# First MLP product with the high and the low part of its input side by side: one matmul of 512 columns and one of 256 in place of three of 256

## The chip, the core and the metric

The kernel runs on one core of a Trainium2 chip. A core has TensorE (matrix products out of SBUF into PSUM), VectorE and ScalarE (elementwise work), GpSimd, and SyncE, whose queue issues most of the loads. PSUM has 8 banks of 512 float32 values per partition. The metric is the device time of one execution in microseconds (us); the median of three runs of the kernel before is 319.94 us (319.66 to 320.01).

## What is computed

One decoder layer on 256 tokens of width 1024: a token mixer of three head groups behind one input projection, an output projection, then an MLP, and a last norm. The part that the change touches is the MLP:

```python
x = x + jnp.einsum('bse,ed->bsd', y, w_out[l])          # x: (1, 256, 1024)
h = rms_norm(x, norm_mlp[l])
u = jnp.square(jax.nn.relu(jnp.einsum('bsd,df->bsf', h, w_ff1[l])))   # w_ff1: (1024, 4096)
x = x + jnp.einsum('bsf,fd->bsd', u, w_ff2[l])          # w_ff2: (4096, 1024)
return rms_norm(x, norm_final)
```

All inputs are float32.

## The kernel before

**Precision.** TensorE multiplies float32 operands in a rounded form (fp32r, one column per cycle). To keep float32 accuracy every operand is split into a high part, rounded to fp32r by a ScalarE copy, and a low part, the difference that VectorE takes and rounds (`split`, lines 70 to 72). A product of two split operands is three matmuls into one PSUM region (`mm3`, lines 299 to 303): high by high, high by low, low by high. The first operand of `T.matmul(o, l, r)` after the output is the stationary one, loaded into the array by a weight load of its own before each matmul; the second is streamed, one column after the other.

**Order of the work.** The order on every engine is the order in which the program issues, written out by hand. The projections run as 84 slots (`slots`), with steps of other engines placed ahead of chosen slots (`plan`, from line 831). Input projection and output projection come first, then the MLP. All weights come in chunks of 128 x 2048 float32 (1 MB). `load` issues a chunk's DMA on SyncE's queue into one of three raw buffers, and `split_w` (line 96) casts half of it on ScalarE (`wh`) and takes the difference on VectorE (`wl`); the second half's split issues the load of three chunks further on. Four buffers each hold `wh` and `wl`.

**The MLP.** `evac_split` (line 171) writes the residual stream, transposed and scaled, as `x1h` and `x1l`: two tiles of 128 x 8 x 256, 8 depth tiles of 256 tokens. The hidden width of 4096 is worked off in 16 chunks of 256. The first product of chunk j (`ff1`, line 785) has, for each of two halves `c` of 128 hidden columns and each depth tile `k`, one `mm3` of 256 columns (`ff1_mm`): weight slice stationary, tokens streamed, both halves into one PSUM bank. `ff1_out` evicts it through `ff1_evac` (line 772): Relu and its Square, rounded to `uh`, on ScalarE, the unrounded square and the difference `ul` on VectorE. The second product (`ff2_mm`) has `uh` and `ul` as stationary operand and 512 columns of a second weight chunk streamed, four accumulators of one bank each held over all chunks. It is 24 matmuls of 512 columns per chunk against 48 of 256 columns in the first product.

Chunk 0 of the first product runs as the last four slots (`ff1_first`, in two banks) while the last transposes and splits of x1 come in; `ff1_first_out` evicts it. Then comes `ff1(1)`, and a loop over j (line 916): second product of j, split of two half chunks, first product of j + 2, split of two more, `ff1_out(j + 2)`. The second products of the last two chunks are done by `last_mm` (line 942) in another order, the last 24 of their matmuls with 256 columns, followed by the residual, the last norm and the stores.

`hTh` and `hTl` (line 155) are the same two parts for the input projection; `x1h` and `x1l` take over their memory.

Of the kernel before, what the change touches and what calls it, by code (L numbers as in the profile page):

```python
# [8 lines left out]
F32 = mybir.dt.float32  # L9
F32R = mybir.dt.float32r  # L10
I32 = mybir.dt.int32
AF = mybir.ActivationFunctionType
OP = mybir.AluOpType
AX = mybir.AxisListType

P = 128
S = 256
D = 1024
KT = D // P
# [13 lines left out]
def trunk_kernel(ctx: ExitStack, tc, x, x_t, w_in, w_out, w_ff1, w_ff2, small, hg_norm, norm_final, out):  # L33
    nc = tc.nc
    V, A, G, T = nc.vector, nc.scalar, nc.gpsimd, nc.tensor
# [12 lines left out]
    def mis(name):  # L48
        b = idle.pop(0)
        held[name] = (b,)  # L50
        return banks[:, b, :]
# [9 lines left out]
    def free(name):  # L61
        idle.extend(held.pop(name))

    def wt(name, shape, tag=None, bufs=None, dt=F32):
        return work.tile(shape, dt, name=name, tag=tag or name, bufs=bufs)

    def flat(t):
        return t.rearrange("p a b -> p (a b)")
# [83 lines left out]
        G.tensor_tensor(r, v, nhalf[:, 0:k], op=OP.pow)  # L152
        return r

    hTh = wt("hTh", [P, KT, S], tag="hTh", dt=F32R)
    hTl = wt("hTl", [P, KT, S], tag="hTl", dt=F32R)
    xsq = wt("xsq", [P, D], tag="yTh")
    gmix = sp[:, SP_GMIX:SP_GMIX + 8]

# [139 lines left out]
    def mm3(o, l, r, first, last):  # L299
        (lh, ll), (rh, rl) = l, r  # L300
        T.matmul(o, lh, rh, start=first, stop=False)  # L301
        T.matmul(o, lh, rl, start=False, stop=False)  # L302
        T.matmul(o, ll, rh, start=False, stop=last)  # L303
# [313 lines left out]
    ps_s, sc_t, nm_t, pr_t, ps_t, PT = {}, {}, {}, {}, {}, {}  # L617
# [110 lines left out]
        ts_ = slice(t * 128, (t + 1) * 128)  # L728
        big_mm(wacc[t, n], yTh[:, k, ts_], yTl[:, k, ts_], NI + k // 2, k % 2, n, k == 0, k == KT - 1)

    x1h = wt("x1h", [P, KT, S], tag="hTh", dt=F32R)
    x1l = wt("x1l", [P, KT, S], tag="hTl", dt=F32R)
    gmlp = sp[:, SP_GMLP:SP_GMLP + 8]
    x1ps = {}
    xt = xa[:, SP_WA:].rearrange("p (t d) -> p t d", t=2)
# [27 lines left out]
    FI = NI + 4  # L763
    uh, ul = {}, {}

    def ff1_mm(o, i, c, k):
        wh = hi_w[i].rearrange("p (k c) -> p k c", c=CW)
        wl = lo_w[i].rearrange("p (k c) -> p k c", c=CW)
        cs = slice(c * 128, (c + 1) * 128)
        mm3(o, (wh[:, k, cs], wl[:, k, cs]), (x1h[:, k, :], x1l[:, k, :]), k == 0, k == KT - 1)  # L770

    def ff1_evac(j, parts):
        r = wt("fr", [P, 512], tag="sc", bufs=3)
        u = wt("fu", [P, 512], tag="pr", bufs=2)
        uh[j] = wt("uh", [P, 512], tag="PT", bufs=8, dt=F32R)
        ul[j] = wt("ul", [P, 512], tag="PT", bufs=8, dt=F32R)
        for src, s_ in parts:
            A.activation(r[:, s_], src, AF.Relu)  # L778
            A.activation(uh[j][:, s_], r[:, s_], AF.Square)
            V.tensor_tensor(u[:, s_], r[:, s_], r[:, s_], op=OP.mult)  # L780
            V.tensor_tensor(ul[j][:, s_], u[:, s_], uh[j][:, s_].bitcast(F32), op=OP.subtract)

    ff1_ps = {}

    def ff1(j, i):
        ps = ff1_ps[j] = mis(f"f{j}")
        for c in range(2):
            for k in range(KT):
                ff1_mm(ps[:, c * 256:(c + 1) * 256], i, c, k)

    def ff1_out(j):
        ff1_evac(j, [(ff1_ps[j], slice(0, 512))])
        free(f"f{j}")

    facc = {}

# [4 lines left out]
        big_mm(facc[t, n], uh[j][:, cs], ul[j][:, cs], i, kk, n, j == 0 and kk == 0,  # L801
               (t, n) == (1, 1) and j == NF - 3 and kk == 1)

    f0 = {}

    def ff1_first(c, kg):
        if kg == 0:
            f0[c] = mis(f"f0{c}")[:, 0:256]
        for k in range(4 * kg, 4 * kg + 4):
            ff1_mm(f0[c], FI, c, k)  # L810

    def ff1_first_out():
        ff1_evac(0, [(f0[c], slice(c * 256, (c + 1) * 256)) for c in range(2)])
        free("f00")
        free("f01")

    def x1_ss():
        for t in range(2):
# [9 lines left out]
    slots += [(wout_part, k, t, n) for k in range(4) for t, n in tn]  # L828
    slots += [(wout_part, k, t, n) for t, n in tn for k in range(4, 8)]
    slots += [(ff1_first, c, kg) for kg in range(2) for c in range(2)]  # L830
    plan = {
        0: [(S_, 0, 0, 4), (x_split, 0), (x_split, 1)],
# [67 lines left out]
    for n, slot in enumerate(slots):  # L900
        for step in plan.get(n, ()):
            step[0](*step[1:])
        slot[0](*slot[1:])
    ff1_first_out()
    S_(FI + 2, 0)
    S_(FI + 2, 1)
    ff1(1, FI + 1)
    S_(FI + 3, 0)
    S_(FI + 3, 1)
    ff1_out(1)  # L910
    x1_ss()
    nc.sync.dma_start(nfb, bass.AP(tensor=norm_final.tensor, offset=norm_final.offset, ap=[[0, P], [1, D]]))
    i = FI + 2
    tnt = sorted(tn)
    tail = {}
    for j in range(NF):
        if j < NF - 2:
            for kk in range(2):
                for t, n in tnt:
                    ff2_mm(j, i, kk, t, n)  # L920
        else:
            tail[j] = i
        split_w(i + 2, 0)
        split_w(i + 2, 1)
        i += 1
        if j + 2 < NF:
            ff1(j + 2, i)
            split_w(i + 2, 0)
            split_w(i + 2, 1)
            ff1_out(j + 2)  # L930
            i += 1
# [136 lines left out]
```

## Time and profile before

| | before |
|---|---|
| median of 3 runs | 319.94 us (319.66 to 320.01) |
| the profiled execution's own time | 319.74 us |
| its span, first to last instruction | 318.0 us |
| mean granted TensorE clock | 0.995 of 2.4 GHz |
| TensorE matmul busy | 309.8 us (97%) |
| VectorE busy | 191.3 us (60%) |
| ScalarE busy | 171.9 us (54%) |

The profile is of one execution. Its times are microseconds from the start of the span unless marked ns. PE is TensorE's matmul, PEld its weight load, DVE is VectorE, ACT is ScalarE, SP is SyncE. L301 is line 301 of the kernel. Since most matmuls and splits go through helpers, their line is the helper's, and the tile names tell the stage: `banks<-x1h,wh` is the first product of the MLP, `banks<-wh,uh` the second, `banks<-wh,yTh` the output projection. Matmuls overlap in the pipeline and their ends are modelled, so the pace of a stretch is read from the starts.

### The profile page before, as it was taken

The numbers are of one execution on the slowest core, as the hardware profiler recorded it, in microseconds if no ns is written. First come the engines' busy times: TensorE is split into PE (matmuls) and PEld (weight loads), VectorE is DVE, ScalarE is ACT, GpSimd is POOL, SyncE is SP. The second block draws the span as 40 slices with busy tenths as digits, with TensorE's granted clock in tenths as the row PEclk, the third lists the DMA queues.
The fourth block names the chain that finished last, engine by engine and source line by source line (L and its number), as shares of the span: only waits on it lengthen the run. The fifth ranks groups of instructions, "written<-read, shape, count | busy, mean of one in ns | idle before, by whom it ended". The sixth has DMA issues, their size and how long they took to land.

```text
span 318.0 us, 5290 instructions
## 1 busy us (share of the span) xinstructions
PE 309.8 (97%) x2164; PEld 284.6 (89%) x2164; DVE 191.3 (60%) x287; ACT 171.9 (54%) x283; POOL 36.4 (11%) x83
## 2 busy tenths in 40 slices
PE   8999999999999999999999999999999999999991
PEld 7999999998999888999899889889989988988981
DVE  1848999983545493697635733753663573375363
ACT  3869699684595360686632652562463264256131
POOL 8328900021410000000000000000000000000000
PEclk9999999999999999999999999999999999999997
DMA  7996553360046346058566246337426624630003
GB/s 199 403 376 253 189 211 132 134 235 31 2 143 255 133 139 260 0 188 343 212 250 248 81 200 265 125 141 266 182 93 255 243 84 203 264 120 15 0 6 128
DMA packets 9961, 55.71 MB, mean 175 GB/s; under 512 B 1232, under 2 KB 1488, under 8 KB 4048
## 3 DMA queue, kind: packets, MB, share of 16 engines
q1 hardware_dynamic: 9216, 54.06, 45.3%
q10 hardware_dynamic: 720, 1.31, 1.3%
q8 instruction: 17, 0.28, 0.3%
q14 instruction: 8, 0.07, 0.1%
HBM read 54.32 MB, written 1.05 MB: 174 GB/s over the span
## 4 chain that ended last, share of the span: by engine, by line
PE 93%; DMA 2%; issue 2%; DVE 1%; ACT 0%; POOLq 0%; POOL 0%; ACTq 0%; DVEq 0%
PE banks L301 28%; PE banks L302 28%; PE banks L303 28%; PE banks L405 2%; DMA raw<-in_w_in_dram 2%; PE banks L641 1%; PE banks L659 1%; PE banks L168 1%; PE banks L676 1%; PE banks L675 1%; PE banks L458 1%; PE banks L521 1%; PE banks L674 1%; DVE xa L957 0%; PE banks L461 0%
## 5 line engine op out<-in xcount | busy, mean ns | idle before, releaser
L72 DVE TENSOR_TENSOR wl<-raw,wh 128x1024 fp32r<-128x1024 f32 (+1 forms) x100 | 113.4, 1181 | 20.1 <-ACT wh L71 18.5
L71 ACT CAST wh<-raw 128x1024 fp32r<-128x1024 f32 (+1 forms) x100 | 95.3, 1010 | 4.1 <-DMA raw<-in_w_in_dram 4.0
L301 PE MATMUL banks<-x1h,wh 128*128 128x256 f32 x256 | 72.4, 283 | 0.0
L302 PE MATMUL banks<-x1l,wh 128*128 128x256 f32 x256 | 72.4, 283 | 0.0
L303 PE MATMUL banks<-x1h,wl 128*128 128x256 f32 x256 | 72.4, 283 | 0.0
L778 ACT ACTIVATE fr<-banks 128x512 f32<-128x512 f32 (+1 forms) x17 | 9.7, 573 | 87.2 <-PE banks L303 87.2
L780 DVE TENSOR_TENSOR fu<-fr 128x512 f32<-128x512 f32 (+1 forms) x17 | 11.2, 659 | 69.5 <-ACT fr L778 69.5
L302 PE MATMUL banks<-wl,uh 128*128 128x512 f32 (+1 forms) x132 | 51.4, 389 | 0.0
L301 PE MATMUL banks<-wh,uh 128*128 128x512 f32 (+1 forms) x132 | 51.3, 389 | 0.0
L303 PE MATMUL banks<-wh,ul 128*128 128x512 f32 (+1 forms) x132 | 51.3, 389 | 0.0
L301 PEld LDWEIGHTS banks<-x1h,wh 128*128 128x128 f32 x256 | 49.0, 191 | 0.7
L302 PEld LDWEIGHTS banks<-x1l,wh 128*128 128x128 f32 x256 | 48.9, 191 | 0.7
L303 PEld LDWEIGHTS banks<-x1h,wl 128*128 128x128 f32 x256 | 49.0, 191 | 0.0
L301 PE MATMUL banks<-hTh,wh 128*128 128x256 f32 x128 | 37.7, 295 | 0.0
L302 PE MATMUL banks<-hTl,wh 128*128 128x256 f32 x128 | 36.6, 286 | 0.3 <-DVE hTl L162 0.3
L303 PE MATMUL banks<-hTh,wl 128*128 128x256 f32 x128 | 36.3, 284 | 0.0
L303 PEld LDWEIGHTS banks<-wh,ul 128*128 128x128 f32 x132 | 24.9, 188 | 5.7
L301 PEld LDWEIGHTS banks<-wh,uh 128*128 128x128 f32 x132 | 24.9, 189 | 5.0
L302 PEld LDWEIGHTS banks<-wl,uh 128*128 128x128 f32 x132 | 24.8, 188 | 5.1
L302 PEld LDWEIGHTS banks<-hTl,wh 128*128 128x128 f32 x128 | 24.6, 192 | 0.8 <-DVE hTl L162 0.8
L301 PEld LDWEIGHTS banks<-hTh,wh 128*128 128x128 f32 x128 | 24.6, 192 | 0.6 <-ACT hTh L161 0.2
L303 PEld LDWEIGHTS banks<-hTh,wl 128*128 128x128 f32 x128 | 24.6, 192 | 0.2 <-DVE wl L72 0.2
(198 smaller groups left out, 417.0 us busy)
## 6 DMA issues: line engine op xcount, KB each, us to landing
raw<-in_w_ff_dram SPq DMA_DIRECT2D x32, 1024.0 KB, 5.0
raw<-in_w_in_dram SPq DMA_DIRECT2D x10, 1024.0 KB, 5.9
raw<-in_w_out_dram SPq DMA_DIRECT2D x4, 1024.0 KB, 4.8
raw<-in_w_in_dram ACTq DMA_DIRECT2D x4, 256.0 KB, 7.3
xtok<-in_x_dram SPq DMA_DIRECT2D x2, 512.0 KB, 8.6
xa<-in_x_dram SPq DMA_DIRECT2D x2, 512.0 KB, 6.2
xa<-in_x_t_dram SPq DMA_DIRECT2D x3, 256.0 KB, 6.2
raw<-in_w_in_dram SPq DMA_DIRECT2D x2, 256.0 KB, 8.0
```

The costliest lines, as they stand in the source:

```text
L71: A.copy(hi, src)
L72: V.tensor_tensor(lo, src, hi.bitcast(F32), op=OP.subtract)
L168: T.transpose(pair[n % 2][:, i * 256 + t * 128:i * 256 + (t + 1) * 128], src[:, t, (k0 + n) * P:(k0 + n + 1) * P], ident)
L301: T.matmul(o, lh, rh, start=first, stop=False)
L302: T.matmul(o, lh, rl, start=False, stop=False)
L303: T.matmul(o, ll, rh, start=False, stop=last)
L405: T.matmul(ps[:, par, g * 64:(g + 1) * 64], kB[r, hp, hs], rhs, start=True, stop=True)
L458: T.matmul(dst, att_d[:, (hp * 2 + half) * 2 + par, :], bv[:, half, h * 64:h * 64 + 64], start=True, stop=(half == 0))
L521: T.matmul(ps[:, c * 256:(c + 1) * 256], spw[:, wofs + c * 128:wofs + (c + 1) * 128], xc[:, c, :], start=True, stop=True)
L641: T.matmul(ps_s[2 * pair + par][:, os], q[r, c, qs], k[r, c, ks], start=True, stop=True)
L778: A.activation(r[:, s_], src, AF.Relu)
L780: V.tensor_tensor(u[:, s_], r[:, s_], r[:, s_], op=OP.mult)
```

## The change

One tile holds the high and the low part of each depth tile next to each other: 128 x 8 x 2 x 256, for the input projection's `hT` and for the MLP's `x1c`; the old names become views of it. `ff1_mm` then needs two matmuls: the weight slice's high part against 512 columns (high and low tokens) into a whole bank, and its low part against the 256 high columns into the bank's first half. The product is the sum of the bank's two halves. `ff1_out` therefore copies the second half to SBUF on ScalarE and adds the first half to it on VectorE, for each of the two banks that a chunk now takes; VectorE computes max(s, 0) x s in one instruction, ScalarE rounds it to `uh`, VectorE takes the difference `ul`. Chunk 0 uses the same functions.

```diff
-    hTh = wt("hTh", [P, KT, S], tag="hTh", dt=F32R)
-    hTl = wt("hTl", [P, KT, S], tag="hTl", dt=F32R)
+    hT = wt("hT", [P, KT, 2, S], tag="hT", dt=F32R)
+    hTh, hTl = hT[:, :, 0, :], hT[:, :, 1, :]
...
-    x1h = wt("x1h", [P, KT, S], tag="hTh", dt=F32R)
-    x1l = wt("x1l", [P, KT, S], tag="hTl", dt=F32R)
+    x1c = wt("x1c", [P, KT, 2, S], tag="hT", dt=F32R)
+    x1h, x1l = x1c[:, :, 0, :], x1c[:, :, 1, :]
...
-        mm3(o, (wh[:, k, cs], wl[:, k, cs]), (x1h[:, k, :], x1l[:, k, :]), k == 0, k == KT - 1)
-
-    def ff1_evac(j, parts):
-        r = wt("fr", [P, 512], tag="sc", bufs=3)
-        u = wt("fu", [P, 512], tag="pr", bufs=2)
+        T.matmul(o, wh[:, k, cs], flat(x1c[:, k]), start=k == 0, stop=False)
+        T.matmul(o[:, 0:S], wl[:, k, cs], x1h[:, k, :], start=False, stop=k == KT - 1)
+
+    ff1_ps = {}
+
+    def ff1_out(j):
+        b = wt("fb", [P, 2, S], tag="sc", bufs=3)
+        s_ = wt("fs", [P, 2, S], tag="pr", bufs=2)
+        u = wt("fu", [P, 512], tag="sc", bufs=3)
         uh[j] = wt("uh", [P, 512], tag="PT", bufs=8, dt=F32R)
         ul[j] = wt("ul", [P, 512], tag="PT", bufs=8, dt=F32R)
-        for src, s_ in parts:
-            A.activation(r[:, s_], src, AF.Relu)
-            A.activation(uh[j][:, s_], r[:, s_], AF.Square)
-            V.tensor_tensor(u[:, s_], r[:, s_], r[:, s_], op=OP.mult)
-            V.tensor_tensor(ul[j][:, s_], u[:, s_], uh[j][:, s_].bitcast(F32), op=OP.subtract)
-
-    ff1_ps = {}
+        for c in range(2):
+            A.copy(b[:, c, :], ff1_ps[j, c][:, S:])
+        for c in range(2):
+            V.tensor_tensor(s_[:, c, :], ff1_ps[j, c][:, 0:S], b[:, c, :], op=OP.add)
+            free(f"f{j}{c}")
+        V.scalar_tensor_tensor(u, flat(s_), 0.0, flat(s_), op0=OP.max, op1=OP.mult)
+        A.copy(uh[j], u)
+        V.tensor_tensor(ul[j], u, uh[j].bitcast(F32), op=OP.subtract)
+
+    def ff1_part(j, i, c, ks):
+        if ks[0] == 0:
+            ff1_ps[j, c] = mis(f"f{j}{c}")
+        for k in ks:
+            ff1_mm(ff1_ps[j, c], i, c, k)
 
     def ff1(j, i):
-        ps = ff1_ps[j] = mis(f"f{j}")
-        for c in range(2):
-            for k in range(KT):
-                ff1_mm(ps[:, c * 256:(c + 1) * 256], i, c, k)
-
-    def ff1_out(j):
-        ff1_evac(j, [(ff1_ps[j], slice(0, 512))])
-        free(f"f{j}")
+        for c in range(2):
+            ff1_part(j, i, c, range(KT))
...
     def ff1_first(c, kg):
-        if kg == 0:
-            f0[c] = mis(f"f0{c}")[:, 0:256]
-        for k in range(4 * kg, 4 * kg + 4):
-            ff1_mm(f0[c], FI, c, k)
-
-    def ff1_first_out():
-        ff1_evac(0, [(f0[c], slice(c * 256, (c + 1) * 256)) for c in range(2)])
-        free("f00")
-        free("f01")
+        ff1_part(0, FI, c, range(4 * kg, 4 * kg + 4))
...
-    ff1_first_out()
+    ff1_out(0)
```

## Rows read from the trace of the kernel before

**Rows 1.** Page, part 1: engines' busy time, share of the span, instructions.
```profile
PE 309.8 (97%) x2164; PEld 284.6 (89%) x2164; DVE 191.3 (60%) x287; ACT 171.9 (54%) x283; POOL 36.4 (11%) x83
```

**Rows 2.** Page, part 4: the chain that ended last, shares by line.
```profile
PE banks L301 28%; PE banks L302 28%; PE banks L303 28%; PE banks L405 2%; DMA raw<-in_w_in_dram 2%; PE banks L641 1%; PE banks L659 1%; PE banks L168 1%; PE banks L676 1%; PE banks L675 1%; PE banks L458 1%; PE banks L521 1%; PE banks L674 1%; DVE xa L957 0%; PE banks L461 0%
```

**Rows 3.** Stages: length, busy PE, PEld, DVE, ACT, POOL; clock, DMA, GB/s.
```profile
152.52:158.13 5.61, 5.61 (x26) 4.52 (x25) 4.56 (x5) 5.02 (x6) 0.00 (x0) 1.00 0.41 171
158.13:163.88 5.75, 5.75 (x50) 5.75 (x49) 1.45 (x2) 0.00 (x0) 0.00 (x0) 1.00 0.94 362
141.16:300.20 159.04, 159.04 (x1011) 143.69 (x1010) 85.94 (x88) 72.47 (x88) 0.00 (x0) 1.00 0.48 182
```

**Rows 4.** Timeline, PE, one MLP round: start, duration; first of ff2, ff1, ff2.
```profile
152.52 0.39 PE L301 MATMUL banks<-wh,uh 128*128 128x512 f32 x1
...
158.13 0.28 PE L301 MATMUL banks<-x1h,wh 128*128 128x256 f32 x1
...
163.88 0.39 PE L301 MATMUL banks<-wh,uh 128*128 128x512 f32 x1
```

**Rows 5.** Timeline, PE, output projection: first and last of ten matmuls.
```profile
113.80 0.39 PE L302 MATMUL banks<-wl,yTh 128*128 128x512 f32 x1
...
115.84 0.39 PE L302 MATMUL banks<-wl,yTh 128*128 128x512 f32 x1
```

**Rows 6.** Timeline, PE, last stage: first and last of nine 256 wide matmuls.
```profile
308.63 0.28 PE L301 MATMUL banks<-wh,uh 128*128 128x256 f32 x1
...
309.56 0.28 PE L303 MATMUL banks<-wh,ul 128*128 128x256 f32 x1
```

**Rows 7.** Groups by line and shape: count | busy us, mean ns | idle before.
```profile
L778 ACT ACTIVATE fr<-banks 128x512 f32<-128x512 f32 x15 | 9.0, 598 | 87.2 <-PE banks L303 87.2
L779 ACT ACTIVATE uh<-fr 128x512 fp32r<-128x512 f32 x15 | 9.5, 634 | 0.5
L780 DVE TENSOR_TENSOR fu<-fr 128x512 f32<-128x512 f32 x15 | 10.4, 691 | 69.5 <-ACT fr L778 69.5
L781 DVE TENSOR_TENSOR ul<-fu,uh 128x512 fp32r<-128x512 f32 x15 | 10.4, 693 | 1.6
L71 ACT CAST wh<-raw 128x512 fp32r<-128x512 f32 x8 | 4.8, 613 | 2.9 <-DMA raw<-in_w_in_dram 2.8
L347 DVE TENSOR_TENSOR sig_f<-banks,RB 128x256 f32<-128x256 f32 x2 | 0.8, 419 | 2.3 <-ACT RB L236 2.3
L541 DVE SCALAR_TENSOR_TENSOR su<-su,th 128x512 f32<-128x512 f32 x1 | 0.7, 691 | 0.2 <-ACT su L540 0.2
```

**Rows 8.** Timeline, ACT and DVE, one round: start, us, [idle before, releaser].
```profile
164.08 0.60 ACT L778 ACTIVATE fr<-banks 128x512 f32<-128x512 f32 x1 [6.31 <-PE banks L303]
...
165.24 3.89 ACT L71 CAST wh<-raw 128x1024 fp32r<-128x1024 f32 x4
...
166.32 4.63 DVE L72 TENSOR_TENSOR wl<-raw,wh 128x1024 fp32r<-128x1024 f32 x4
```

**Rows 9.** Timeline, start of the MLP: DVE, PE and ACT around chunk 0.
```profile
132.69 0.88 DVE L176 SCALAR_TENSOR_TENSOR x1l<-banks,xa,x1h 128x256 fp32r<-128x256 f32 x2 [0.15 <-ACT x1h L175]
...
133.58 0.28 PE L301 MATMUL banks<-x1h,wh 128*128 128x256 f32 x1
133.69 0.32 PE L302 MATMUL banks<-x1l,wh 128*128 128x256 f32 x1
133.85 0.28 PE L303 MATMUL banks<-x1h,wl 128*128 128x256 f32 x1
...
134.84 0.38 ACT L778 ACTIVATE fr<-banks 128x256 f32<-128x256 f32 x1
...
138.02 4.62 DVE L72 TENSOR_TENSOR wl<-raw,wh 128x1024 fp32r<-128x1024 f32 x4
```

**Rows 10.** Timeline, tail: DVE's `ul` of the last chunk, PE's first reader.
```profile
301.82 0.69 DVE L781 TENSOR_TENSOR ul<-fu,uh 128x512 fp32r<-128x512 f32 x1
...
303.48 0.39 PE L303 MATMUL banks<-wh,ul 128*128 128x512 f32 x1
```

More of the change, by code (lines that the diff above doesn't have):

```diff
@@ L802, in ff2_mm @@
                (t, n) == (1, 1) and j == NF - 3 and kk == 1)
-    f0 = {}
     def ff1_first(c, kg):
-        if kg == 0:
-            f0[c] = mis(f"f0{c}")[:, 0:256]
-        for k in range(4 * kg, 4 * kg + 4):
-            ff1_mm(f0[c], FI, c, k)
-    def ff1_first_out():
-        ff1_evac(0, [(f0[c], slice(c * 256, (c + 1) * 256)) for c in range(2)])
-        free("f00")
-        free("f01")
+        ff1_part(0, FI, c, range(4 * kg, 4 * kg + 4))
     def x1_ss():
```

## The prediction

> **What bounds the kernel now.** I read the page's engine totals first: TensorE is busy for 97% of the span, no other compute engine for more than 60% [rows 1]. A busy TensorE need not be the bound, so the chain of waits comes next: 84% of it are the three matmul lines of `mm3`, and no VectorE or ScalarE line carries more than 1% [rows 2]. Third, the table by stage. From 141.16 to 300.20 us, the fourteen rounds of the MLP, TensorE is busy for all 159.04 us, VectorE for 54% and ScalarE for 46%; the granted clock is 1.00 there, which is the upper level of 2.4 GHz. Within one round of 11.36 us the second product (ff2) takes 5.61 us and the first (ff1) 5.75 us [rows 3]. So ff1, which alone changes its matmuls, is set by TensorE's own pace, and there a saved nanosecond is a saved nanosecond.
>
> The pace is read from starts, not from durations, since matmuls overlap. From 158.13 to 163.88 lie 48 matmuls of 256 columns, 119.8 ns each. From 152.52 to 158.13 lie 24 of 512 columns, 233.8 ns each [rows 4]. At 2.4 GHz 256 columns are 106.7 ns and 512 are 213.3 ns, so a matmul costs 13.1 ns beyond its columns in ff1 and 20.5 ns in ff2. Two other stretches show that this surplus isn't one constant. In the output projection 9 intervals of 512 columns last from 113.80 to 115.84, 226.7 ns each, a surplus of 13.3 ns [rows 5]; in the last stage 8 intervals of 256 columns take 0.93 us, 116 ns each, a surplus of 10 ns [rows 6]. ff1 and the output projection agree on 13.3 ns per matmul whatever its width; the two stretches that load their stationary operand from `uh` and `ul` don't fit it.
>
> **The change part by part.** *Matmuls of ff1.* For each of 16 chunks, 2 column halves and 8 depth tiles, three matmuls of 256 columns become one of 512 and one of 256. The 768 columns stay; one matmul and one weight load go, 256 times in all. Now a set costs 3 x 119.8 = 359.4 ns. The 512 wide matmul with a weight slice as stationary operand isn't in this trace. The nearest rows give it 226.7 ns [rows 5] or 233.8 ns [rows 4]; its outer bound is twice a 256 wide one, 239.6 ns. The 256 wide one is between 116 and 119.8 ns [rows 4, 6]. I take 226.7 + 119.8 = 346.5 ns, since ff1 is already one of the stretches with the even surplus of 13.3 ns: a saving of 12.9 ns per set. The ends are 226.7 + 116 = 342.7 (16.7 saved) and 239.6 + 119.8 = 359.4 (nothing saved).
>
> *Start of ff1.* The first matmul of a set now reads both halves of x1, so it needs VectorE's low part, which so far only the second needed. The critical one is the last depth tile: VectorE ends it at 133.57 (132.69 + 0.88), and the matmul that reads it starts at 133.69 and is held a little (0.32 us long where its neighbours have 0.28) [rows 9]. Now the first matmul of that tile starts at 133.58. Afterwards the whole set has to wait until about 133.70, then runs 0.35 us to 134.05; before, the third matmul of that set starts at 133.85 and is through its columns and surplus by 133.97. So the saving of the twelve sets ahead is lost in that wait and 0.08 us with it; the four sets left of chunk 0 give 0.05 us back. Chunk 0 brings nothing (-0.03 us), and 15 chunks x 16 sets = 240 sets count: 240 x 12.9 ns = 3.1 us.
>
> *Eviction.* Before, ScalarE takes Relu (0.598 us) and Square (0.634), VectorE a product (0.691) and a difference (0.693) [rows 7]. Afterwards ScalarE copies two halves out of PSUM (0.38 each by the 256 wide Relu [rows 9]) and writes the rounded part (0.613); VectorE adds twice (0.419 each, the row that reads PSUM and SBUF), squares behind the maximum (0.691) and subtracts (0.693) [rows 7]. That is 0.14 us more for ScalarE and 0.84 us more for VectorE per chunk. The chain from the last matmul to `ul` grows from 0.60 + 0.69 + 0.69 = 1.98 to 0.38 + 0.42 + 0.69 + 0.61 + 0.69 = 2.79 us, with two more handovers some 0.9 us; the first half's copy and sum run while TensorE works on the second. ScalarE now waits inside the chain for VectorE's square, and queued behind it are the casts of the next two chunks, behind those VectorE's differences, and behind those SP's loads. What covers this: ScalarE is idle for 6.31 us per round, waiting for TensorE, and VectorE's four differences end at 170.95 (166.32 + 4.63), with the next ff2, which reads the first two, at 163.88 + 11.36 = 175.24, and TensorE needs `uh` a whole ff2 and ff1 (11 us) after it is asked for [rows 4, 8]. So 0.9 us costs nothing in the rounds. If the cover were gone, it would cost 0.9 us per round, 13 us in all.
>
> The cover is thin twice. At chunk 0, VectorE's four differences start at 138.02 [rows 9], behind an eviction of four 256 wide instructions (4 x 0.42, so it began near 136.3). Afterwards, from 136.3 on, the sums and the square (1.53 us) have to end, then ScalarE's copy (0.61) and one cast (about 1 us, four take 3.89 [rows 8]), before the first difference can start, near 139.5. It belongs to ff2's first weight chunk and then ends near 140.7, where it now ends near 139.2 (a fourth of 4.62). ff2 begins near 141.0 and reads it with its second matmul 0.23 us later: covered by some 0.5 us, cost 0, at the other end 0.3 us. In the tail, `ul` of the last chunk is ready at 302.51 and its first reader starts at 303.48 [rows 10]. With 0.9 us more it lands at 303.4, while its weights are loaded one matmul ahead: I take 0.15 us of wait, between 0 and 0.3.
>
> *Banks and buffers.* A chunk takes two PSUM banks instead of one: four of ff2 and two for each of two chunks are eight, and a bank is written again 11 us after its sums. No cost; without that distance TensorE would wait for the eviction chain, 2.8 us per round. One tile for both parts of h and x1 doubles the step between depth tiles and leaves the input projection's 576 matmuls as they are. If addresses decided the surplus, their 120 ns could move to the 116 of [rows 6] (2.3 us less) or by as much the other way; I take 0, because each matmul still reads the same 256 neighbouring elements.
>
> **Sum.** 3.1 - 0.03 - 0.15 = 2.9 us. The profiled execution took 319.74 us with a span of 318.0 us; it lies 0.2 us under the median of 319.94, and what lies around the span doesn't change. 319.94 - 2.9 = 317.0 us.
>
> **The rivals.**
> *Wide like ff2.* The 512 wide matmul costs 233.8 ns as in ff2, the set 353.6, the saving is 240 x 5.8 = 1.4 us: 318.7 us. For it: ff2 is the neighbouring stage, with the same weight tiles and the same traffic around it. Against it: the odd surplus goes with `uh` and `ul` as stationary operand, which ff1 doesn't have.
> *Short narrow one.* Behind a wide matmul the weights for the narrow one are loaded early and it costs 116 ns; saving 240 x 16.7 = 4.0 us: 316.1 us. For it: in [rows 3] weight loads fill all of ff1 (5.75 of 5.75 us) and 4.52 of 5.61 us of ff2, so ff1's 120 ns may partly be load.
> *The surplus goes with the columns, hardly with the matmul.* Then 768 columns cost what they cost, and with the tail's 0.2 us the time is 319.5 to 320.1. For it: ff2's wide matmul has 1.6 times the surplus of ff1's narrow one. Against it: [rows 5].
> Beside that row stands a rule against this change: the Trainium skill, "TensorE: Matmul & The Clock Gate", section "Back-to-back issue gap", gives a warm matmul N/2.4 + 2.5 ns. By it a dropped matmul is worth 2.5 ns, 240 of them 0.6 us, and an estimate from that page would be 319.5 us. The trace has five times that surplus in both stretches of even pace, so the row decides.
> *Slower.* The wide matmul in ff1 pays the surplus of its columns (2 x 13.1) and on top of it the 7.1 ns by which ff2's exceeds the output projection's: 213.3 + 26.2 + 7.1 = 246.6, a set 366.4 ns, 240 x 7.0 = 1.7 us lost and the tail's wait: 321.8 us. Place: every set of ff1; it decides from a wide matmul of 239.6 ns upward. Against it: no 512 wide row is as long.
>
> **How the numbers follow.** Forecast 55%, its own range 316.4 to 317.6 (sets of 344 to 349 ns). Wide like ff2 20%, 318.0 to 319.0. Short narrow one 11%. Surplus with the columns 8%. Slower 6%. The range of 315.4 to 319.0 takes in the first three and the thin covers, and leaves out the last two and the lower edge of the third. A measurement of this kernel can tell 0.2% (0.64 us) from no change: faster 0.86, within 0.2% 0.08, slower 0.06.
>
> **What would show it.** In the changed kernel's timeline a set of ff1 should repeat every 346 ns, wide to narrow 227 and narrow to wide 120, ff1 of a round take 5.54 us instead of 5.75, and ff2 stay at 5.61. ScalarE's idle time per round should stay above 4 us and end on TensorE. In the tail `ul` should come about 3.2 us after ff1's end instead of 2.3. The forecast is wrong if the wide matmul takes over 233 ns, if TensorE shows a gap at the start of ff2 in any round, or if the input projection's pace moves from 120 ns.

## The result and the profile after

The changed kernel takes 318.02 us (median of 4 runs, 317.64 to 318.18) against 319.98 us before (4 runs, 319.66 to 320.24). The ratio is 0.9934, 95% interval 0.9922 to 0.9947: 1.96 us faster. The forecast was 317.0 us, 2.9 us faster, with a range of 315.4 to 319.0. The direction is right and the time lies in the range; the gain is two thirds of the one forecast, and 318.02 us lies at the lower edge of what the rival "wide like ff2" was given (318.0 to 319.0), not in the forecast's own 316.4 to 317.6.

| | before | after |
|---|---|---|
| profiled execution, its span | 319.74, 318.0 us | 317.64, 315.9 us |
| first matmul of the MLP to the last matmul of the kernel | 182.11 us | 180.28 us |
| a round's ff1 (chunks 2 to 15) | 5.745 us, all alike | 5.558 us in five rounds, 5.64 to 5.65 in nine |
| a round's ff2 | 5.615 us | 5.614 to 5.621 us |

Of the 2.1 us between the two spans, 1.83 us lie in the MLP. The other 0.28 us are there before the MLP begins; 0.24 of them have arisen by the third split matmul of the kernel, behind the arrival of the first weights (ScalarE's first cast of them starts at 5.34 us before and at 5.17 after). These rows are of TensorE's timeline (start, duration), before and after; the starts are equal up to 6.59 us.

```profile
7.13 0.55 PE L302 MATMUL banks<-hTl,wh 128*128 128x256 f32 x1
7.51 0.29 PE L303 MATMUL banks<-hTh,wl 128*128 128x256 f32 x1
```

```profile
7.05 0.39 PE L302 MATMUL banks<-hT,wh 128*128 128x256 f32 x1
7.27 0.28 PE L303 MATMUL banks<-hT,wl 128*128 128x256 f32 x1
```

That wait differs between executions of other kernels too (in the runs below that change nothing ahead of the MLP, it begins anywhere from 128.9 to 130.3 us), so stages are compared by their own lengths here.

Two rounds of the changed kernel on TensorE, first matmul of ff1, ff2, ff1, ff2:

```profile
157.72 0.40 PE L770 MATMUL banks<-x1c,wh 128*128 128x512 f32 x1
...
163.27 0.39 PE L301 MATMUL banks<-wh,uh 128*128 128x512 f32 x1
...
168.90 0.39 PE L770 MATMUL banks<-x1c,wh 128*128 128x512 f32 x1
...
174.54 0.39 PE L301 MATMUL banks<-wh,uh 128*128 128x512 f32 x1
```

They answer [rows 4]. The first ff1 takes 5.55 us, as forecast (5.54). The second, with the same 32 instructions, takes 5.64. Inside them the starts go like this; first some of the short round, then of the long one:

```profile
160.15 0.39 PE L770 MATMUL banks<-x1c,wh 128*128 128x512 f32 x1
160.38 0.28 PE L771 MATMUL banks<-x1c,wl 128*128 128x256 f32 x1
160.50 0.39 PE L770 MATMUL banks<-x1c,wh 128*128 128x512 f32 x1
...
171.01 0.40 PE L770 MATMUL banks<-x1c,wh 128*128 128x512 f32 x1
171.24 0.28 PE L771 MATMUL banks<-x1c,wl 128*128 128x256 f32 x1
171.35 0.40 PE L770 MATMUL banks<-x1c,wh 128*128 128x512 f32 x1
171.59 0.28 PE L771 MATMUL banks<-x1c,wl 128*128 128x256 f32 x1
171.71 0.40 PE L770 MATMUL banks<-x1c,wh 128*128 128x512 f32 x1
171.95 0.28 PE L771 MATMUL banks<-x1c,wl 128*128 128x256 f32 x1
172.07 0.40 PE L770 MATMUL banks<-x1c,wh 128*128 128x512 f32 x1
```

In the short round a set takes 0.35 us from the second on (346.7 ns: 230 and 117). In the long one the sets go round in threes, 1.06 us for three (wide 233, 236, 241 ns, narrow 117, 113, 120), 353.3 ns each. So the same instructions run in two lasting patterns, neither with the 227 and 120 ns that the prediction added up. Short rounds come every third time.

The eviction is as sized. Its groups (count | busy, mean ns | idle before, releaser), which answer [rows 7]:

```profile
L782 ACT COPY fb<-banks 128x256 f32<-128x256 f32 x32 | 11.8, 371 | 62.5 <-PE banks L771 62.5
L784 DVE TENSOR_TENSOR fs<-banks,fb 128x256 f32<-128x256 f32 x32 | 13.3, 423 | 42.9 <-ACT fb L782 42.9
L787 ACT CAST uh<-fu 128x512 fp32r<-128x512 f32 x16 | 9.9, 620 | 22.6 <-DVE fu L786 22.6
```

### The profile page after: what moved, and what is told of

Its sections match the earlier page's. It is cut to its first block, busy times and chain, and to the rows that moved or that the text cites. A ratio compares the mean times of both kernels' runs of the same rounds, so it can differ in the third digit from the quotient of the medians.

```text
span 315.9 us, 4816 instructions
## 1 busy us (share of the span) xinstructions
PE 307.5 (97%) x1908; PEld 270.7 (86%) x1908; DVE 204.5 (65%) x317; ACT 173.6 (55%) x297; POOL 36.4 (12%) x83
## 4 chain that ended last, share of the span: by engine, by line
PE 93%; DMA 2%; issue 2%; DVE 1%; ACT 1%; POOLq 0%; POOL 0%; ACTq 0%; DVEq 0%
PE banks L770 19%; PE banks L301 19%; PE banks L302 18%; PE banks L303 18%; PE banks L771 10%; PE banks L405 2%; DMA raw<-in_w_in_dram 2%; PE banks L641 1%; PE banks L659 1%; PE banks L168 1%; PE banks L676 1%; PE banks L675 1%; PE banks L458 1%; PE banks L521 1%; PE banks L674 1%
## 5 line engine op out<-in xcount | busy, mean ns | idle before, releaser
L770 PE MATMUL banks<-x1c,wh 128*128 128x512 f32 x256 | 90.9, 397 | 0.0
L771 PE MATMUL banks<-x1c,wl 128*128 128x256 f32 x256 | 71.8, 281 | 0.0
L770 PEld LDWEIGHTS banks<-x1c,wh 128*128 128x128 f32 x256 | 48.0, 188 | 11.7 <-DVE x1c L176 0.2
L771 PEld LDWEIGHTS banks<-x1c,wl 128*128 128x128 f32 x256 | 48.3, 189 | 0.7
L782 ACT COPY fb<-banks 128x256 f32<-128x256 f32 x32 | 11.8, 371 | 62.5 <-PE banks L771 62.5
L784 DVE TENSOR_TENSOR fs<-banks,fb 128x256 f32<-128x256 f32 x32 | 13.3, 423 | 42.9 <-ACT fb L782 42.9
L301 PE MATMUL banks<-hT,wh 128*128 128x256 f32 x128 | 37.5, 293 | 0.0
L302 PE MATMUL banks<-hT,wh 128*128 128x256 f32 x128 | 36.4, 284 | 0.5 <-DVE hT L162 0.5
L303 PE MATMUL banks<-hT,wl 128*128 128x256 f32 x128 | 36.3, 283 | 0.0
L302 PEld LDWEIGHTS banks<-hT,wh 128*128 128x128 f32 x128 | 24.5, 191 | 1.0 <-DVE hT L162 0.9
L301 PEld LDWEIGHTS banks<-hT,wh 128*128 128x128 f32 x128 | 24.6, 192 | 0.5
L303 PEld LDWEIGHTS banks<-hT,wl 128*128 128x128 f32 x128 | 24.5, 191 | 0.1
```

Source lines behind the costliest of these rows:

```text
L770: T.matmul(o, wh[:, k, cs], flat(x1c[:, k]), start=k == 0, stop=False)
L771: T.matmul(o[:, 0:S], wl[:, k, cs], x1h[:, k, :], start=False, stop=k == KT - 1)
L782: A.copy(b[:, c, :], ff1_ps[j, c][:, S:])
L784: V.tensor_tensor(s_[:, c, :], ff1_ps[j, c][:, 0:S], b[:, c, :], op=OP.add)
```

## The experiments

Four theories were carried through. A: a wide matmul of ff1 has a fixed price, whatever runs around it. B: the surplus over the columns comes from where the operands lie in SBUF. C: an even stretch of one width settles at a surplus of 13.3 ns, and a change of width starts it anew. D, a form of B: what counts is where the stationary tile lies against the streamed one within 256 bytes of a partition. The expectations use the letter A in more than one way: in that of e1 it is C with the settled pace from the first matmul on, in those of e3 and e4 a fixed price of every matmul, and e5 calls the fixed price "the count alone". A set is one wide and one narrow matmul; "round" is a round of the MLP loop, ff1 and ff2 are its two products.

| run | ff1 per round, us | ff2 per round, us | MLP to the end, us | ratio to before, 95% interval |
|---|---|---|---|---|
| before | 5.745 | 5.615 | 182.11 | |
| after | 5.558 (5 rounds), 5.64 to 5.65 (9) | 5.614 to 5.621 | 180.28 | 0.9934 (0.9922 to 0.9947) |
| e2_three | 5.745 | 5.615 | 182.13 | 0.9990 (0.9979 to 1.000) |
| e1_grouped | 5.598 | 5.615 | 180.33 | 0.9943 (0.9921 to 0.9964) |
| e3_align_all | 5.555 (2), 5.644 (12) | 5.562 (5.58 and 5.60 in the first two) | 179.80 | 0.9918 (0.9897 to 0.9938) |
| e4_u_moved | 5.644 | 5.562 | 179.95 | 0.9924 (0.9904 to 0.9944) |
| e5_wide16 | 5.578 | 5.615 | 179.65 | 0.9931 (0.9916 to 0.9946) |
| e6_ff2_order | as after | as after | 180.28 | 0.9935 (0.9918 to 0.9952) |
| e7_extra | 5.664 (7), 5.762 (7) | 5.609 to 5.621 | 181.67 | one run, 319.21 us |
| e8_one_tile | as after | as after | 180.09 | one run, 317.65 us |
| e9_u_160 | 5.640 | 5.467 | 178.46 | 0.9908 (0.9880 to 0.9937) |
| e10_wide16_u160 | 5.539 | 5.468 | 176.96 | 0.9848 (0.9833 to 0.9862) |
| e11_before_u160 | 5.752 | 5.468 | 179.97 | 0.9939 (0.9924 to 0.9954) |
| e12_x_128 | 5.601 | 5.473 | 177.94 | one run, 315.12 us |

The column before the last runs from the first matmul of the MLP to the last of the kernel, in the profiled execution. It leaves out the waits ahead of the MLP, which move its beginning by as much as 1.3 us between runs with the same program up to there.

**e2_three: the change without the matmul that it saves.**

```diff
-        T.matmul(o, wh[:, k, cs], flat(x1c[:, k]), start=k == 0, stop=False)
+        T.matmul(o[:, 0:S], wh[:, k, cs], x1h[:, k, :], start=k == 0, stop=False)
+        T.matmul(o[:, S:], wh[:, k, cs], x1l[:, k, :], start=False, stop=False)
         T.matmul(o[:, 0:S], wl[:, k, cs], x1h[:, k, :], start=False, stop=k == KT - 1)
```

> The changed kernel with the three matmuls of 256 columns per set back in ff1, high by low now into the bank's second half; the tile with both parts side by side and the new eviction stay. This is the change without the matmul that it saves. If eviction and layout are covered, as the prediction has it, ff1 takes 5.75 us per round as before, the tail loses at most 0.15 us, and the ratio to before is 1.000. If the longer eviction or the new layout costs something, it shows here alone: 0.9 us per round would be 1.04, a shifted pace of the input projection up to 0.993 or 1.007.

```profile
169.66 0.28 PE L770 MATMUL banks<-x1c,wh 128*128 128x256 f32 x1
...
175.40 0.39 PE L301 MATMUL banks<-wh,uh 128*128 128x512 f32 x1
```

48 matmuls in 5.74 us, as before in every round, and 0.02 us more for the MLP as a whole. The tile with both parts and the longer eviction cost nothing that shows. What the change gains is the pace of its two matmuls against three.

**e1_grouped and e5_wide16: wide and narrow not in turn.** In e1 each column half runs its eight wide, then its eight narrow matmuls; in e5 both halves' sixteen wide come first, then the sixteen narrow. First the loop of e1, then that of e5:

```diff
-        for k in ks:
-            ff1_mm(ff1_ps[j, c], i, c, k)
+        for wide in (True, False):
+            for k in ks:
+                ff1_mm(ff1_ps[j, c], i, c, k, wide)
```

```diff
+        for wide in (True, False):
+            for c in range(2):
+                for k in range(KT):
+                    ff1_mm(ff1_ps[j, c], i, c, k, wide)
```

> The changed kernel with the order inside ff1 changed alone: per column half first the eight matmuls of 512 columns, then the eight of 256, instead of wide and narrow in turn. Theory A (a surplus of 13.3 ns per matmul wherever a stretch runs in one width, and the turn of widths spoils it): wide intervals of 227 ns as in the output projection, narrow of 120, a round of ff1 5.55 us against 5.56 or 5.65 in the changed kernel, and all fourteen rounds alike; 0.9 us faster than the changed kernel, ratio to before 0.9905. Theory B (the surplus depends on where the operands lie, not on the order): wide intervals stay between 230 and 241 ns with a mean near 234, no faster than the changed kernel.

> The changed kernel; in the chunks from 1 on ff1 takes the sixteen wide matmuls of both column halves first, then the sixteen narrow ones (in the run before it was eight and eight per half, and its wide intervals came down from 233 to 227 ns after some five matmuls, its narrow ones up to 120 after two). Theory C (the pace settles: an even stretch of one width comes to 13.3 ns of surplus after a few matmuls, each change of width starts anew): one settling less per round, wide intervals 232 for five and 227 for eleven, a round of ff1 5.56 us against 5.60 with eight and eight, all rounds alike, and the whole 0.5 us faster than that run and 0.6 to 0.9 us faster than the changed kernel. Theory of the count alone (a fixed price per wide matmul in ff1, 234 ns): 5.65 us and no faster than the changed kernel.

TensorE's timeline of a column half in e1 and of a round in e5 (rows of one kind are merged, x8 is eight matmuls, and their pace is the distance to the next row; the narrow x5 and the last x2 are cut off by the end of the view):

```profile
170.44 2.02 PE L771 MATMUL banks<-x1c,wh 128*128 128x512 f32 x8
172.29 1.11 PE L773 MATMUL banks<-x1c,wl 128*128 128x256 f32 x8
173.24 0.63 PE L771 MATMUL banks<-x1c,wh 128*128 128x512 f32 x2
```

```profile
170.07 3.83 PE L771 MATMUL banks<-x1c,wh 128*128 128x512 f32 x16
173.74 0.76 PE L773 MATMUL banks<-x1c,wl 128*128 128x256 f32 x5
...
175.65 0.39 PE L301 MATMUL banks<-wh,uh 128*128 128x512 f32 x1
```

Eight wide ones take 231 ns each, sixteen 229. The single intervals of e5 are 233, 236, 224, 231, 236, 228, 233, 231, and then 226 to 227 for the rest; the narrow ones reach 120 after two. All rounds are alike. That is theory C, with eight matmuls until it settles where five were expected (5.578 us instead of 5.56); theory A would have left 234 and 5.65. The 5.55 us expected of e1 was missed for the same reason (5.598): a stretch of eight settles only at its end. On the MLP e5 gains 0.63 us over the changed kernel, within the 0.6 to 0.9 expected; e1 gains nothing over it (180.33 against 180.28), since its chunk 0, grouped by fours among the last transposes, takes 6.61 us instead of 6.25. The ratios don't separate e5 from the changed kernel: their intervals overlap, and in e5's profiled execution the MLP began 1.3 us later.

**e7_extra and e8_one_tile: what picks the pattern.** e7 puts one small matmul ahead of each ff1. e8 reads the same depth tile eight times, so its product is another one.

```diff
+        T.matmul(ps[:, 0:64], wh[:, 0, 0:128], x1h[:, 0, 0:64], start=True, stop=True)
```

```diff
-        T.matmul(o, wh[:, k, cs], flat(x1c[:, k]), start=k == 0, stop=False)
-        T.matmul(o[:, 0:S], wl[:, k, cs], x1h[:, k, :], start=False, stop=k == KT - 1)
+        T.matmul(o, wh[:, 0, cs], flat(x1c[:, 0]), start=k == 0, stop=False)
+        T.matmul(o[:, 0:S], wl[:, 0, cs], x1h[:, 0, :], start=False, stop=k == KT - 1)
```

> The changed kernel with one small matmul of 64 columns more at the start of each ff1 from chunk 1 on, into a bank that the next matmul starts anew. It costs some 0.11 us per round by itself, the point is the pattern: in the changed kernel five of fourteen rounds take 5.56 us (sets of 346.7 ns) and the others 5.64 (sets of 353.3), every third one being short. If the moment at which ff1 is entered picks the pattern, other rounds become short, or all or none, while sets stay at one of these two values. If something that turns with three buffers picks it, the same third of the rounds stays short, all being 0.11 us longer.

> The changed kernel with ff1 reading the same depth tile, weights and x, eight times in each column half (the product is therefore another; seven eighths of the operands are left out, all instructions stay). If the step from depth tile to depth tile, an address, made the intervals of a set go round in three (241, 236, 233), they become all alike here. If the pattern is one of time, intervals and the two lengths of a round stay as in the changed kernel.

Two rounds of e7, first matmul of ff1, ff2, ff1, ff2:

```profile
169.27 0.19 PE L799 MATMUL banks<-x1c,wh 128*128 128x64 f32 x1
...
175.03 0.39 PE L301 MATMUL banks<-wh,uh 128*128 128x512 f32 x1
...
180.65 0.19 PE L799 MATMUL banks<-x1c,wh 128*128 128x64 f32 x1
...
186.31 0.39 PE L301 MATMUL banks<-wh,uh 128*128 128x512 f32 x1
```

5.76 and 5.66 us: now every second round is short, not every third, and the sets inside keep to the two patterns. So the pattern is picked at the entry into ff1, not by a buffer that turns in threes. The other runs agree: where every ff2 has one length, every ff1 has one too (e4, e9), and in e3 the two short rounds are those behind an ff2 of another length (5.60 and 5.58 us). What in the entry picks it was not isolated. e8 has the rounds of the changed kernel to 2 ns (5.557, 5.642, 5.647), so the step from depth tile to depth tile, a multiple of 1 KB, plays no part. Its MLP is 0.19 us shorter because chunk 0, which reads depth tile 0 alone, doesn't wait for the last parts of x1 (6.07 us instead of 6.25).

**e6_ff2_order: ff2's order as in the output projection.**

```diff
-    tnt = sorted(tn)
+    tnt = tn
```

> The changed kernel with one word changed: ff2 goes over its four accumulators in the order in which the output projection does, so that two sets in a row share the streamed weights and not the stationary u. ff1 is left as it is. If the order of the operands is why the output projection settles at 226.7 ns and ff2 does not, ff2 falls from 5.61 to 5.44 us per round and the whole is 2.5 us faster than the changed kernel (ratio to before 0.986). If the place of u decides, ff2 stays at 5.61 and the ratio at 0.993 to 0.994.

Every round has the length that it has in the changed kernel, 5.614 to 5.621 us for ff2. The order of ff2's operands isn't what keeps it from 227 ns.

**e3_align_all, e4_u_moved, e9_u_160, e11_before_u160: where the operands lie.** In the kernels before and after, the addresses in a partition leave these remainders of 256 bytes: weights, x and y 224, the tiles u (high and low) 64. A wider small tile ahead moves them; the diff is that of e9 and e11, e4 has 16 columns there instead of 48, and e3 has these 16 and a constant's tile of 16 columns instead of 8. e3 brings weights, x and y to 0 and u to 128; e4 moves u alone by 32 bytes, to 96; e9 and e11 move it by 160, to 224, the remainder of the weights, e9 in the changed kernel and e11 in the one before.

```diff
-        lbe, lbr = sa["lbe"], wt("sp0", [P, 2])
+        lbe, lbr = sa["lbe"], wt("sp0", [P, 48])[:, 0:2]
```

> The changed kernel with two small tiles made larger, nothing else. In the changed kernel the weights, both x tiles and the y tiles start 32 bytes past a multiple of 64 bytes within a partition, and the tiles u (high and low) on a multiple of 64; here all of them start on a multiple of 64. Theory A (the surplus is a fixed price of a matmul) and a theory of the order alone: every pace stays, ratio to before 0.993 to 0.994. Theory B (the surplus comes from where the operands lie; an operand that starts half way needs one piece more, and 16 columns are 6.7 ns): the surplus of the input projection and of the output projection falls from 13.3 ns to 7 or less, 1,150 and more matmuls get shorter by at least 6 ns, and the kernel is faster than the changed one by 7 us or more, ratio to before below 0.975.

> The changed kernel with one small tile made larger so that the tiles u (high and low) start 32 bytes past a multiple of 64 bytes, as weights, x and y do in it; nothing else moves that TensorE reads in the MLP. Theory A: ff2 stays at 234 ns per matmul, ratio 0.993 to 0.994. Theory B in its form that only the difference between the two operands of a matmul counts: ff2 falls to 226.7 ns as in the output projection, 5.44 us per round instead of 5.61, and the whole is 2.5 us faster than the changed kernel, ratio 0.986. Theory B in its form that every operand off the multiple of 64 costs: ff2 gets slower or stays.

> The changed kernel with the tiles u (high and low) moved by 160 bytes, so that they start at the same remainder of 256 bytes as the weights (224), as the y tiles of the output projection do. A move by 32 bytes, to a difference of 128, took ff2 from 5.61 to 5.56 us per round and made every round of ff1 a long one. Theory D (ff2's surplus depends on the place of its stationary tile against the streamed one; at the same remainder it settles like the output projection): ff2 at 227 ns per matmul, 5.44 to 5.46 us per round, and the whole 2.2 us or more faster than the changed kernel, ratio to before 0.986. If the place within 256 bytes isn't what the output projection has ahead of ff2: 5.56 to 5.65 us per round, ratio 0.992 to 0.995.

> The kernel before with u moved by 160 bytes. Theory D: ff2 falls as in the changed kernel, to 5.44 to 5.46 us per round, ff1 stays at 5.75 (120 ns per matmul), the whole is 2.3 us faster than the kernel before, ratio 0.993; the change is then worth, beside the run of it with the same move, the same 0.10 to 0.19 us per round. If ff2 doesn't fall, ratio 1.000.

First the ff2 of one round in e4, then in e9 with two settled matmuls between its ends, then a whole round of e11:

```profile
175.21 0.39 PE L301 MATMUL banks<-wh,uh 128*128 128x512 f32 x1
...
180.78 0.39 PE L770 MATMUL banks<-x1c,wh 128*128 128x512 f32 x1
```

```profile
174.59 0.40 PE L301 MATMUL banks<-wh,uh 128*128 128x512 f32 x1
...
177.33 0.39 PE L301 MATMUL banks<-wh,uh 128*128 128x512 f32 x1
177.56 0.39 PE L302 MATMUL banks<-wl,uh 128*128 128x512 f32 x1
...
180.05 0.39 PE L770 MATMUL banks<-x1c,wh 128*128 128x512 f32 x1
```

```profile
169.01 0.28 PE L301 MATMUL banks<-x1h,wh 128*128 128x256 f32 x1
...
174.76 0.40 PE L301 MATMUL banks<-wh,uh 128*128 128x512 f32 x1
...
180.23 0.28 PE L301 MATMUL banks<-x1h,wh 128*128 128x256 f32 x1
```

e3 refutes B in its absolute form: with all operands on a multiple of 64 bytes, the input and the output projection keep 120 and 227 ns, and the kernel isn't 7 us faster. Nor does every pace stay, as theory A had it: ff2 falls to 5.56 us. In e4 u and the weights have the same remainder of 64 bytes and of 128, and ff2 misses the 5.44 us expected of equal places, so equality within 128 bytes isn't enough. e3 and e4 share one thing, a difference of 128 between u and the weights, and they share ff2's 5.56 us. With a difference of 0 ff2 starts at 233, 236, 228, 232, 231 and then settles at 227 like the output projection: 5.47 us, theory D, with 0.01 us more than its expectation. The whole of e9 fell short of it (0.9908 against 0.986): ff2 gives 2.1 us, but all rounds of ff1 are long now, which takes 0.4 back. e11 shows that ff2's part of it has nothing to do with the change: the kernel before gains as much from 160 bytes (0.9939) as from the change (0.9934).

**e10_wide16_u160: the edits of e5 and e9 together.**

> Sixteen wide matmuls, then sixteen narrow ones, in ff1, and u moved by 160 bytes: the two edits together, the version that should beat both kernels. Theory D with the settling of theory C: ff1 5.56 to 5.58 us and ff2 5.44 to 5.46 us per round, 14 rounds of 11.02 instead of 11.24 us in the changed kernel, some 3 us faster than it, 315 us, ratio to before 0.984. If the move does nothing for ff2, 0.992.

```profile
168.74 0.39 PE L771 MATMUL banks<-x1c,wh 128*128 128x512 f32 x1
...
174.28 0.40 PE L301 MATMUL banks<-wh,uh 128*128 128x512 f32 x1
...
179.74 0.39 PE L771 MATMUL banks<-x1c,wh 128*128 128x512 f32 x1
...
298.55 0.49 PE L303 MATMUL banks<-wh,ul 128*128 128x512 f32 x1
```

314.81 us, ratio 0.9848: it beats both kernels, by 3.3 us the MLP of the changed one (176.96 against 180.28). ff1 takes 5.54 us: coming from a settled ff2, its wide matmuls are at 227 from the first on. The last row is the first reader of `ul` of the last chunk: 0.49 us long where its neighbours have 0.39, and 331 ns to the next start instead of 227, so the tail waits 0.10 us now that ff2 runs faster ahead of it.

**e12_x_128: the tile of both parts moved by 128 bytes against the weights**, on top of e9.

```diff
+        m = wt(name, [P, KT * 2 * S + 64], tag="hT", dt=F32R)
+        return m[:, 32:32 + KT * 2 * S].rearrange("p (k h t) -> p k h t", k=KT, h=2)
```

> The changed kernel with u moved by 160 bytes as in the run before it (wide and narrow in turn, sets of 353 ns in every round, ff2 settled at 227), and with the tile of both parts, of h and of x1 alike, moved by 128 bytes against the weights within 256. Theory D taken to all stages: the input projection, whose streamed or stationary tile now lies 128 off, leaves its settled 120 ns (the 512 wide case went from 227 to 232 at that difference), and the sets of ff1 change their length away from 353.3 too; ff2 and the output projection stay at 227. If the turn of widths alone makes ff1's sets long, they stay at 346.7 or 353.3; if only u's place was special, the input projection stays at 120.

A round's ff1 and ff2, then ten intervals of the input projection:

```profile
168.24 0.40 PE L774 MATMUL banks<-x1c,wh 128*128 128x512 f32 x1
...
173.84 0.40 PE L305 MATMUL banks<-wh,uh 128*128 128x512 f32 x1
```

```profile
11.09 0.28 PE L305 MATMUL banks<-hT,wh 128*128 128x256 f32 x1
...
12.28 0.28 PE L306 MATMUL banks<-hT,wh 128*128 128x256 f32 x1
```

The input projection leaves its even 120 and goes round in 115, 117, 122, 120, 119, some 119 ns on average, and the sets of ff1 take 350 ns. Theory D holds for all stages, with a sign that was not expected: in stretches of one width narrow matmuls get a little shorter off the weights' remainder, wide ones longer. The wider tile also pushes u, and the high part of y, on by 256 bytes, and ff2 and the output projection still settle at 227.

## Why the prediction was right or wrong, point by point

- **The bound.** Right. ff1 shortened by its matmuls' pace, the kernel by ff1, and e2 shows that nothing else of the change moves the time clear of noise.
- **The price of a set.** This is the step that was mis-sized. Forecast: 226.7 + 119.8 = 346.5 ns in all 240 sets, a saving of 12.9 ns each, 3.1 us. Measured: sets of 346.7 ns in five rounds, of 353 ns in nine and in chunk 1. Those ten chunks have 160 sets 6.3 ns dearer than forecast, 1.0 us of the 1.1 us between the 2.9 us forecast and the 1.83 us gained in the MLP; the smaller differences (a tail 0.14 us better than forecast, each other stage up to 0.07 us worse) nearly cancel. The rival "wide like ff2" (353.6 ns, 318.7 us) has the sum of these ten chunks, the forecast that of the other five, and the time lies between the two. Both have it by luck: measured are 230 + 117 in short rounds and 237 + 117 on average in long ones, against 226.7 + 119.8 and 233.8 + 119.8. The narrow one at 117 is what the rival "short narrow one" said, but not with its wide one. In the long rounds the prediction's own sign of being wrong came, a wide matmul over 233 ns.
- **Why.** The reading that 13.3 ns is a matmul's surplus "whatever its width" was a reading of settled stretches. e5 and e10 show that it holds there for the wide matmul of ff1 too (227 ns). In turn with narrow ones it doesn't settle at 227 and 120, but falls into one of two patterns (in e12 into a third, of 350 ns a set), and e7 shows that the entry picks which. What makes the two widths disturb each other was not found. In settled stretches the count argument is exact: from e11 to e10 a round's ff1 goes from 5.752 to 5.539 us, 13.3 ns for each of 16 sets.
- **The sentence that the surplus goes with `uh` and `ul`.** Half right: it goes with where they lie. e9 moved them and ff2 settled. The 116 ns that the prediction read from [rows 6] is 117 over the whole stretch; the rows give starts to 0.01 us only.
- **The place as a term taken at 0.** "Each matmul still reads the same 256 neighbouring elements" was the right value for the wrong reason. The change moved no tile by a part of 256 bytes, so the input projection kept 120 ns; e12 shows that a move of 128 takes it off that, and where the prediction gave the place at most 2.3 us, that move is worth 0.6 (576 matmuls, 118.7 ns on average against 119.7).
- **The start.** Chunk 0 was forecast to lose 0.03 us; from its first matmul to chunk 1's it takes 6.25 us instead of 6.19. The wait for the last parts of x1 is spread over three matmuls, and e8 puts it at 0.18 us. The thin cover behind chunk 0 held: VectorE's first difference starts at 139.11 us (forecast 139.5), and ff2 begins at 140.84 without a wait. The durations show two of the three matmuls, 0.50 and 0.44 us where others have 0.40:

```profile
132.93 0.50 PE L770 MATMUL banks<-x1c,wh 128*128 128x512 f32 x1
133.27 0.28 PE L771 MATMUL banks<-x1c,wl 128*128 128x256 f32 x1
133.39 0.44 PE L770 MATMUL banks<-x1c,wh 128*128 128x512 f32 x1
```

- **The eviction in the rounds.** Right at no cost. ScalarE is idle for 4.9 us in the round shown, above the 4 us named as the sign, but not all of it ends on TensorE: 1.22 us are the wait for VectorE's square inside the chain. Its casts come after that, still far ahead of their use:

```profile
160.70 0.37 ACT L782 COPY fb<-banks 128x256 f32<-128x256 f32 x1 [1.24 <-PE banks L771]
163.47 0.37 ACT L782 COPY fb<-banks 128x256 f32<-128x256 f32 x1 [2.40 <-PE banks L771]
165.06 0.62 ACT L787 CAST uh<-fu 128x512 fp32r<-128x512 f32 x1 [1.22 <-DVE fu L786]
165.59 3.90 ACT L71 CAST wh<-raw 128x1024 fp32r<-128x1024 f32 x4
```

- **The tail.** `ul` ends 3.13 us after ff1 does (300.51 + 0.69 - 298.07; forecast 3.2, before 2.3 [rows 10]). The wait was taken at 0.15 us and is 0.01: its first reader, at 301.35, is 0.41 us long instead of 0.40. The cover was that thin all the same, as e10 shows with 0.10 us.

```profile
300.51 0.69 DVE L788 TENSOR_TENSOR ul<-fu,uh 128x512 fp32r<-128x512 f32 x1 [0.69 <-ACT uh L787]
...
301.35 0.41 PE L303 MATMUL banks<-wh,ul 128*128 128x512 f32 x1
```

- **The rule of a small fixed part.** The Trainium skill, "TensorE: Matmul & The Clock Gate", section "Back-to-back issue gap", has N/2.4 + 2.5 ns for a warm matmul, and calls it the gap of an isolated one. No stretch of these runs of rounded float32 matmuls, each with a weight load of its own, comes to it: settled intervals are 120 and 227 ns, 13.3 above the columns. An estimate of the saving from that page would have been 0.6 us; the MLP gained 1.83.

## What to carry to other kernels

One matmul fewer for the same columns was worth 13.3 ns where the stream had settled, and 8 ns on average where two widths took turns (6 in the long rounds): put matmuls of one width behind each other, sixteen rather than eight, before counting on the settled pace. Read a surplus over N columns from intervals in sequence, not from a mean, and ask first whether the stretch has settled. Compare the addresses of the stationary and the streamed tile within 256 bytes when two stages of one shape run at different pace; here 160 bytes of padding were worth as much as the whole change, and the change, the grouping by width and the padding together took 1.5% off.

## What the runs showed of the hardware that was not expected

In stretches of one width, where stationary and streamed tile have the same remainder of 256 bytes, matmuls of 512 columns come to 226.7 ns and those of 256 to 120.0. With 128 bytes between them it is 232 ns (e4) and 118.7 (e12), with 96 between them 234 (before, ff2) and 117 (before, last stage), always in a pattern that repeats after a few matmuls. Only these three differences were run. That it is the remainder of 256 bytes rests on two runs: equality within 128 wasn't enough (e4), and 256 bytes more changed nothing (e12). Why the place matters was not found. After a change of width the wide matmuls took five to eight to settle, the narrow ones two to eight (eight in ff1 of the kernel before, behind its unsettled ff2).
